# A scheduler of deferred VectorE work: a larger credit cap, no limit on tasks abreast, two shifted due times, more identity transposes ahead of the first product

## The chip, the cores and the metric

The kernel runs on one core of a Trainium2 chip. The metric is the device time of one execution in microseconds (us). TensorE (PE) multiplies, VectorE (DVE), ScalarE (ACT) and GpSimd (POOL) work beside it, each through its own queue in program order; PEld is TensorE's loading of weights. A stretch of the trace is given from the start of the profiled span.

## The reference

One encoder block on 256 tokens of width 4096, in float32. All weights are used once.

```
h = rms_norm(x, norm_gain); proj = h @ w_in            # 4096 -> 22528
q, k, v, z_attn, u_four, z_four, gates = split(proj)
o_attn = dilated window attention of 24 heads, merged over 3 groups by their log-sum-exp
branch_attn = (o_attn * silu(z_attn)) @ w_branch_attn  # 1024 -> 4096
y_four = real(fft2(u_four)) over tokens and group channels
branch_four = (y_four * silu(z_four)) @ w_branch_fourier   # 2048 -> 4096
mixed = sigmoid(g_attn) * branch_attn + sigmoid(g_four) * branch_four
out = rms_norm(x + mixed @ w_out, final_norm_gain)
```

## The kernel before, in words

**Products.** Every weight matrix is cut into column blocks of 512 (`gemm`). A block is worked off in steps of two 128-row slices: 16 steps where 4096 rows are summed. For a step, ScalarE copies 128x1024 weights to a rounded high half `wh`, and VectorE subtracts to get the low half `wl` (`split`). TensorE then does 12 products of 128x512 for the step: for each of two slices and two token tiles `wh` by the left side's high half, `wl` by its high half, `wh` by its low half. So each split of VectorE feeds four products with `wl`. Three pairs of `wh` and `wl` buffers rotate; the weights come by 1 MB transfers on SyncE's queue. In this text a **step** is one such split and its 12 products, and steps are counted from the kernel's first split.

**Deferred work.** Everything else that VectorE and ScalarE do (gates, rotary positions, softmax, 32x32 transposes, the folding of the left side for the Fourier branch, merging of the branches, final sums) is written as Python generators, the tasks. A task yields pairs (cost, delay): the VectorE time of its next piece in planned us, and the number of steps after which it may start. `step()`, called once per step between the split of the next step and the products of this one, hands out credit: `BUDGET` 1.45 (0.75 while the Fourier projection is interleaved, `BUDGET_U`), summed up to `CAP`. It walks through the list of tasks and issues pieces while credit lasts. This is done when the program is built: the result is a fixed order in each engine's queue. A piece of VectorE therefore stands between two splits, and all later splits queue behind it.

**Limits.** A task waits for the tasks named in its `after` list. Besides, `clock.abreast` lets the walk look only at so many tasks that are not urgent: 2 at first, 16 from the block `ZA0` to the end of the attention's transposes, 2 again for the merging.

**Due times.** `finish(...)` issues at once all that is left of given tasks. It is called for the attention heads (line 786) before the buffers of the attention are given up, and for the merging tasks within the first block of the last product, at its step 10 (line 865). In the merging stage each of eight column blocks has a block of products with `w_branch_attn` (4 steps) and one with `w_branch_fourier` (8 steps), and per token tile a task `transpose` that adds, transposes (16 instructions of 32x128), and splits the mixed rows `m` into `m_hi` and `m_lo`, which are the left side of the last product.

**Folding.** For the Fourier branch, `fold(b)` works on four 128-row slices of the left side: two pieces `f`, two pieces of an `e` pair, then ScalarE's `f_hi`, then VectorE's `f_lo`. The first three such tasks run before and within the first interleaved steps, five later ones follow further on. The interleaved projection itself adds, in a cycle of three steps, `wo` and `wu`, two `ul`, one `r` on VectorE, and two `uh` on ScalarE.

**Beginning.** Before the first product TensorE runs `warm(n)`: n transposes of an identity into an unused bank. Between them stand the four transposes of the first tiles of `x` and one of the gain.

Of the kernel before, what the change touches and what calls it, by code (L numbers as in the profile page):

```python
# [35 lines left out]
GA = (1, 3)  # L36
BUDGET = 1.45
BUDGET_U = 0.75
CAP = 1.5
ABREAST = 2  # L40
LEAD = 3

Q0, K0, V0, ZA0, U0, ZF0, G0 = 0, 3072, 6144, 9216, 10240, 12288, 14336
# [13 lines left out]
class Clock:  # L57
    now = 0
    budget = BUDGET
    abreast = ABREAST  # L60
    credit = 0.0


# [32 lines left out]
def hybrid_block(ctx: ExitStack, tc: tile.TileContext, x, norm_gain, w_in, gate_bias, w_attn,  # L96
# [3 lines left out]
    w_in, w_attn, w_four, w_out = w_in[0], w_attn[0], w_four[0], w_out[0]  # L100
# [34 lines left out]
    clock = Clock()  # L135
# [11 lines left out]
    def flush():  # L147

        while pending:
            pending.pop()()  # L150

    def finish(these):
        flush()
        complete(these)

    def complete(these):
        for t in list(these):
            complete(t.after)
            while t in tasks:
                if not t.run(clock.now):  # L160
                    tasks.remove(t)

    def step():
        clock.now += 1
        clock.credit = min(clock.credit + clock.budget, CAP)
        others = 0
        for t in list(tasks):
            if not t.urgent:
                others += 1
                if others > clock.abreast:  # L170
                    break
            if any(u in tasks for u in t.after):
                continue
            while t.ready <= clock.now and (t.cost <= clock.credit or clock.credit >= CAP):
                clock.credit -= t.cost
                if not t.run(clock.now):
                    tasks.remove(t)
                    break

    def split(src, hi, lo):  # L180
        act.activation(hi, src, AF.Copy)
        dve.tensor_tensor(lo, src, hi.bitcast(F32), op=ALU.subtract)
# [5 lines left out]
    def blocks(a):  # L188
        return a.rearrange("p (b k) -> p b k", k=P)
# [44 lines left out]
    def turn(name, shape, dtype):  # L234
        n = turns[name] = turns.get(name, -1) + 1
        if name == "wt":
            return wtp.tile(shape, dtype, name=f"wt{n % 3}")
        n %= 3 + len(spare)
        if n < 3:
            return wpool.tile(shape, dtype, name=f"{name}{n}")  # L240
        return lower(2 * spare[n - 3] + (name == "wl"), shape, dtype, f"{name}{n}")

    def gemm(accs, hi, lo, w, c0, lag=0, during=None, loading=None, at=None, between=None):

        nk = w.shape[0] // P
        wv = w[:, c0:c0 + CW].rearrange("(k p) n -> p k n", p=P)
        wt = None
        steps = []  # L250

        def load(k):
            nonlocal wt
            if k >= nk:
                return
            single = loading is not None and k == 0
            if k % WG == 0:
                wt = turn("wt", [P, WG, CW], F32)
                pieces = [(0, WG)] if not single else [(0, 1), (1, 2), (2, WG)]
                for a, b in pieces:  # L260
                    sp.dma_start(wt[:, a:b, :], wv[:, k + a:k + b, :])
                    if loading is not None:
                        loading(k + b)
            wh = turn("wh", [P, WS, CW], F32R)
            wl = turn("wl", [P, WS, CW], F32R)
            for j in range(0, WS, 1 if single else WS):
                n = slice(j, j + (1 if single else WS))
                split(wt[:, k % WG + n.start:k % WG + n.stop, :], wh[:, n], wl[:, n])
            steps.append((wh, wl))

        def multiply(i, j, t):
            if not 0 <= i < len(steps):
                return
            wh, wl = steps[i]
            k = i * WS + j
            a, b = hi[:, k, t * P:(t + 1) * P], lo[:, k, t * P:(t + 1) * P]
            pe.matmul(accs[t], a, wh[:, j, :], start=(k == 0), stop=False)
            pe.matmul(accs[t], a, wl[:, j, :], start=False, stop=False)
            pe.matmul(accs[t], b, wh[:, j, :], start=False, stop=(k == nk - 1))

        def run(i):
            load((i + 1) * WS)
            if during is not None:
                during(i * WS)
            if at is not None and i == at[0]:
                at[1]()
            step()
            for j in range(WS):
                for t in range(NT):
                    multiply(i - lag * t, j, t)  # L290
                if between is not None and j == 0:
                    between(i * WS)

        load(0)
        flush()
        if during is not None:
            during(-WS)
        last = nk // WS + lag - 1
        for i in range(last):
            run(i)  # L300
        pending.append(lambda: run(last))
# [62 lines left out]
    def warm(n):  # L364

        for _ in range(n):
            pe.transpose(idle_ps[:, :P], ident, ident)

    idle_ps = ps_mm.tile([P, CW], F32, name="acc10")
    x_load(0)  # L370
    warm(3)
    x_transposed(0)
    warm(6)

    def x_ahead(k):

# [290 lines left out]
    clock.budget = BUDGET  # L667


    clock.abreast = 16  # L670
    za = [new_accs()]
    gemm(za[0], h_hi, h_lo, w_in, ZA0, during=lambda k: u_hook(k) if k <= 12 else None)
    za.append(new_accs())
# [18 lines left out]
    with ExitStack() as st:  # L692
        ap = pool(st, "ap")
        at = pool(st, "at", bufs=2)
# [100 lines left out]
    with ExitStack() as st:  # L795
        ft = pool(st, "ft2")
        ys = [ft.tile([P, NT, CW], F32, name=f"yb{c}") for c in range(4)]
        for c in range(4):
            nc.gpsimd.dma_start(ys[c], y_d[:, :, c * CW:(c + 1) * CW].rearrange("t p n -> p t n"))

        def transposed(n, src, b, hi, lo):

            yield 0.0, 5 if n >= 4 else 0
            pt = ps_t.tile([P, 2, SEQ], F32, name="pt") if n % 2 else ps_s.tile([P, 2, SEQ], F32, name="sc")
            for j in range(2):
                for t in range(NT):
                    pe.transpose(pt[:, j, t * P:(t + 1) * P], src[:, t, (b + j) * P:(b + j + 1) * P], ident)
            yield 0.0, LEAD
            act.activation(hi, pt, AF.Copy)
            yield 0.7, 1  # L810
            dve.tensor_tensor(lo, pt, hi.bitcast(F32), op=ALU.subtract)

        flat = []
        for hi, lo, srcs in ((a_hi, a_lo, [sz]), (y_hi, y_lo, ys)):
            for k in range(0, hi.shape[1], 2):
                n = hi.shape[1] // len(srcs)
                flat.append(spawn(transposed(len(flat), srcs[k // n], k % n, hi[:, k:k + 2, :], lo[:, k:k + 2, :]),
                                  False, flat[-4:-3]))
        gates(2)
        finish(flat)  # L820
        clock.abreast = ABREAST


    m_hi, m_lo = lhs_parts("m")
    with ExitStack() as st:
        bp = pool(st, "bp", bufs=2)

        def scale_attn(ga, pa):
            for t in range(NT):
                yield 0.75, 0  # L830
                dve.tensor_mul(ga[:, t, 0, :], ga[:, t, 0, :], pa[t])

        def merge(c, ga, pf):
            for t in range(NT):
                yield 0.75, 0
                dve.tensor_mul(ga[:, t, 1, :], ga[:, t, 1, :], pf[t])

        def transpose(c, t, ga):
            yield 0.6, 0
            m = bp.tile([P, CW], F32, name="m")  # L840
            dve.tensor_add(m, ga[:, t, 1, :], ga[:, t, 0, :])
            mT = bp.tile([P, 4, P], F32, name="mT")
            yield from flipped(mT, blocks(m))
            yield from splitting(mT, m_hi[:, 4 * c:4 * c + 4, t * P:(t + 1) * P], m_lo[:, 4 * c:4 * c + 4, t * P:(t + 1) * P])

        merges, merging = [], []
        for c in range(8):
            if c > 2:
                complete(merges[c - 3])

            ga = sz.rearrange("p t (i n) -> p t i n", i=2) if c % 3 == 2 else bp.tile([P, NT, 2, CW], F32, name="ga")
            for i in range(2):
                nc.gpsimd.dma_start(ga[:, :, i, :], gates_d[:, :, i * D + c * CW:i * D + (c + 1) * CW].rearrange("t p n -> p t n"))
            accs = new_accs()
            gemm(accs, a_hi, a_lo, w_attn, c * CW)
            use(scale_attn(ga, accs))
            accs = new_accs()
            gemm(accs, y_hi, y_lo, w_four, c * CW)
            merged = use(merge(c, ga, accs))
            for t in range(NT):  # L860
                merging.append(spawn(transpose(c, t, ga), False, merged + merging[-2:-1]))
            merges.append(merging[-2:])

        first = new_accs()
        gemm(first, m_hi, m_lo, w_out, 0, at=(10, lambda: finish(merging)))

    br_stack.close()

# [108 lines left out]
```

## Time and profile before

| | |
|---|---|
| time, median of 3 | 2556.85 us (2555.99 to 2556.87) |
| profiled execution: its time | 2554.68 us |
| its span | 2552.9 us |
| TensorE busy | 2524.2 us, 99% of the span |
| VectorE busy | 1761.9 us, 69% |
| ScalarE busy | 1127.7 us, 44% |

The span is the profiled part of one execution; 1.8 us of that execution's time lie around it. The profiled execution was 2.2 us under the median of the others. All helper calls have one line in the trace (L54, the wrapper that records them in order), so rows are told apart by the tiles they write and read.

### The profile page before, as it was taken

How to read it: one execution, taken by the hardware profiler on the slowest of the kernel's cores; microseconds unless marked ns; L12 is line 12 of the kernel's file. 1: busy time of each engine (PE TensorE's matmuls, PEld its weight loads, DVE VectorE, ACT ScalarE, POOL GpSimd, SP SyncE). 2: the span in 40 equal slices, each digit the busy share in tenths (PEclk: the TensorE clock that was granted, in tenths of full speed). 3: DMA queues.
4: the chain of work that ended last, by engine and by line, in shares of the span. 5: the costliest groups of instructions: out<-in, count | busy, mean ns of one | idle time of the engine just before them, and what ended most of it. 6: DMA issues, size and time to landing. Idle time of an engine off the chain costs nothing.

```text
span 2552.9 us, 29910 instructions
## 1 busy us (share of the span) xinstructions
PE 2524.2 (99%) x11630; PEld 2103.2 (82%) x11630; DVE 1761.9 (69%) x2532; ACT 1127.7 (44%) x1352; POOL 77.8 (3%) x146
## 2 busy tenths in 40 slices
PE   9999999999999999999999999999999999899998
PEld 7888888888888888888888888888788888688886
DVE  5688877787754675757678775867756888754554
ACT  6645545454444434343444434344444444344443
POOL 0000000000001000000000000000000000000000
PEclk9999999999999999999999999999999999999999
DMA  7767666666655655565555555655666666566674
GB/s 253 249 231 241 237 228 238 235 231 215 222 173 173 202 189 192 198 195 189 186 185 186 189 188 195 198 178 194 229 228 219 207 221 201 174 196 223 218 243 149
DMA packets 252846, 529.60 MB, mean 207 GB/s; under 512 B 9984, under 2 KB 10784, under 8 KB 252704
## 3 DMA queue, kind: packets, MB, share of 16 engines
q1 hardware_dynamic: 237056, 471.89, 55.9%
q0 software_dynamic: 15600, 55.78, 6.5%
q8 instruction: 91, 1.49, 0.2%
q14 instruction: 51, 0.42, 0.0%
q10 hardware_dynamic: 48, 0.02, 0.0%
HBM read 512.97 MB, written 14.68 MB: 207 GB/s over the span
## 4 chain that ended last, share of the span: by engine, by line
PE 97%; DVE 1%; DMA 0%; ACT 0%; issue 0%; SPq 0%; DVEq 0%; ACTq 0%
PE acc L54 91%; PE pt L54 3%; PE sc L54 3%; DMA wt<-in_w_in_dram 0%; DVE mT L54 0%; DVE wl L54 0%; ACT wh L54 0%; DVE pT L54 0%; DVE res L54 0%; DVE h_lo L54 0%; ACT junk L54 0%; DVE m_lo L54 0%; DVE m L54 0%; ACT h_hi L54 0%; SPq L54 0%
## 5 line engine op out<-in xcount | busy, mean ns | idle before, releaser
L54 DVE TENSOR_TENSOR wl<-wt,wh 128x1024 fp32r<-128x1024 f32 (+1 forms) x865 | 1057.0, 1224 | 678.2 <-ACT wh L54 675.9
L54 ACT ACTIVATE wh<-wt 128x1024 fp32r<-128x1024 f32 (+1 forms) x865 | 912.9, 1059 | 1176.2 <-PE acc L54 1118.0
L54 PE MATMUL acc<-wh,h_hi 128*128 128x512 f32 x2560 | 1003.0, 392 | 0.9 <-ACT wh L54 0.9
L54 PE MATMUL acc<-wh,h_lo 128*128 128x512 f32 x2560 | 997.3, 390 | 0.0
L54 PE MATMUL acc<-wl,h_hi 128*128 128x512 f32 x2560 | 997.1, 389 | 0.1
L54 PEld LDWEIGHTS acc<-wh,h_lo 128*128 128x128 f32 x2560 | 481.0, 188 | 100.6
L54 PEld LDWEIGHTS acc<-wh,h_hi 128*128 128x128 f32 x2560 | 481.0, 188 | 97.1 <-ACT wh L54 1.3
L54 PEld LDWEIGHTS acc<-wl,h_hi 128*128 128x128 f32 x2560 | 481.1, 188 | 96.9 <-DVE wl L54 1.3
L54 PE MATMUL acc<-wh,m_hi 128*128 128x512 f32 x512 | 200.3, 391 | 9.2 <-ACT wh L54 9.2
L54 PE MATMUL acc<-wl,m_hi 128*128 128x512 f32 x512 | 200.2, 391 | 0.9 <-DVE wl L54 0.9
L54 PE MATMUL acc<-wh,m_lo 128*128 128x512 f32 x512 | 199.9, 390 | 0.0
L54 PEld LDWEIGHTS acc<-wh,m_hi 128*128 128x128 f32 x512 | 96.6, 189 | 29.6 <-ACT wh L54 9.6
L54 PEld LDWEIGHTS acc<-wl,m_hi 128*128 128x128 f32 x512 | 96.6, 189 | 22.0 <-DVE wl L54 1.8
L54 PEld LDWEIGHTS acc<-wh,m_lo 128*128 128x128 f32 x512 | 96.5, 189 | 20.1
L54 PE MATMUL acc<-wh,y_lo 128*128 128x512 f32 x256 | 101.2, 395 | 0.0
L54 PE MATMUL acc<-wl,y_hi 128*128 128x512 f32 x256 | 100.8, 394 | 0.0
L54 PE MATMUL acc<-wh,y_hi 128*128 128x512 f32 x256 | 100.0, 391 | 0.0
L54 DVE STREAM_TRANSPOSE mT<-m 32x128 f32<-32x128 f32 x256 | 77.4, 303 | 4.1
L54 DVE STREAM_TRANSPOSE pT<-e 32x128 f32<-32x128 f32 x256 | 77.2, 302 | 4.0
L54 DVE TENSOR_TENSOR ul<-wo,uh 128x508 fp32r<-128x508 f32 x64 | 44.0, 687 | 44.5 <-ACT uh L54 44.5
L54 ACT ACTIVATE uh<-wo 128x508 fp32r<-128x508 f32 x64 | 40.3, 630 | 71.4 <-DVE ul L54 71.4
L54 ACT ACTIVATE uh<-wu 128x516 fp32r<-128x516 f32 x64 | 40.9, 639 | 46.1 <-DVE wu L54 23.5
(151 smaller groups left out, 1679.3 us busy)
## 6 DMA issues: line engine op xcount, KB each, us to landing
wt<-in_w_in_dram SPq DMA_DIRECT2D x319, 1024.0 KB, 5.1
wt<-in_w_out_dram SPq DMA_DIRECT2D x64, 1024.0 KB, 5.5
wu<-in_w_in_dram POOLq DMA_DIRECT2D x64, 512.0 KB, 5.3
wt<-in_w_branch_fourier_dram SPq DMA_DIRECT2D x32, 1024.0 KB, 5.4
wt<-in_w_branch_attn_dram SPq DMA_DIRECT2D x16, 1024.0 KB, 5.5
gates_d<-sg POOLq DMA_DIRECT2D x32, 256.0 KB, 4.2
ga<-gates_d POOLq DMA_DIRECT2D x12, 512.0 KB, 5.3
bias<-in_gate_bias_dram SPq DMA_DIRECT2D x16, 256.0 KB, 5.5
```

The costliest lines, as they stand in the source:

```text
L54: return lambda *a, **k: self.tc.keep_in_program_order(f(*a, **k))
```

## The change

The credit of a step is kept up to 2.7 instead of 1.5. The limit on tasks abreast is gone: only the `after` lists hold a task back. The transposes of the Fourier rows become due 8 steps after they are spawned instead of 5. The forced end of the merging tasks stands at step 13 of the first block of the last product instead of step 10. At the beginning 14 and 40 identity transposes stand where 3 and 6 stood.

```
-CAP = 1.5
-ABREAST = 2
+CAP = 2.7
...
     budget = BUDGET
-    abreast = ABREAST
     credit = 0.0
...
         clock.credit = min(clock.credit + clock.budget, CAP)
-        others = 0
         for t in list(tasks):
-            if not t.urgent:
-                others += 1
-                if others > clock.abreast:
-                    break
             if any(u in tasks for u in t.after):
                 continue
             while t.ready <= clock.now and (t.cost <= clock.credit or clock.credit >= CAP):
...
     x_load(0)
-    warm(3)
+    warm(14)
     x_transposed(0)
-    warm(6)
+    warm(40)
...
-    clock.abreast = 16
...
-            yield 0.0, 5 if n >= 4 else 0
+            yield 0.0, 8 if n >= 4 else 0
...
-        clock.abreast = ABREAST
...
-        gemm(first, m_hi, m_lo, w_out, 0, at=(10, lambda: finish(merging)))
+        gemm(first, m_hi, m_lo, w_out, 0, at=(13, lambda: finish(merging)))
```

VectorE's queue, in the first block of the last product, from step 748 on (`wl` is a split, `mT` a transpose of merged rows), before:

```order
L54 TENSOR_TENSOR wl_16853<-wt_16850,wh_16852 128x1024
L54 STREAM_TRANSPOSE mT<-m 32x4x32 x4
L54 TENSOR_TENSOR wl_16873<-wt_16850,wh_16872 128x1024
L54 TENSOR_TENSOR m_lo<-mT,m_hi 128x4x128
L54 TENSOR_TENSOR m<-ga 128x512
L54 STREAM_TRANSPOSE mT<-m 32x4x32 x16
L54 TENSOR_TENSOR m_lo<-mT,m_hi 128x4x128
L54 TENSOR_TENSOR m<-ga 128x512
L54 STREAM_TRANSPOSE mT<-m 32x4x32 x16
L54 TENSOR_TENSOR m_lo<-mT,m_hi 128x4x128
L54 TENSOR_TENSOR wl_16935<-wt_16932,wh_16934 128x1024
```

The same place with the change:

```order
L53 TENSOR_TENSOR wl_16922<-wt_16899,wh_16921 128x1024
L53 STREAM_TRANSPOSE mT<-m 32x4x32 x4
L53 TENSOR_TENSOR wl_16944<-wt_16941,wh_16943 128x1024
L53 TENSOR_TENSOR wl_16961<-wt_16941,wh_16960 128x1024
L53 TENSOR_TENSOR m_lo<-mT,m_hi 128x4x128
L53 TENSOR_TENSOR wl_16980<-wt_16977,wh_16979 128x1024
```

Of the forced piece between two splits (32 transposes, two sums, three `m_lo`) one `m_lo` is left; the rest stands in earlier steps.

VectorE's queue at the end of the attention, steps 608 to 610 (`pT` is a transpose of the softmax rows, `e`, `mx`, `nm` the masked scores and their maximum), before:

```order
L54 TENSOR_TENSOR wl_13890<-wt_13887,wh_13889 128x1024
L54 STREAM_TRANSPOSE pT<-e_6789 32x4x32 x4
L54 TENSOR_TENSOR wl_13910<-wt_13887,wh_13909 128x1024
L54 STREAM_TRANSPOSE pT<-e_6789 32x4x32 x4
L54 TENSOR_TENSOR e_6790<-sc,mask_t 128x512
L54 TENSOR_REDUCE mx<-e_6790 128x1
L54 TENSOR_SCALAR nm<-mx 128x1
L54 SCALAR_TENSOR_TENSOR sz<-pt,rden_6795,sz 128x128
L54 RECIPROCAL rden_6796<-den_6793 128x1
L54 STREAM_TRANSPOSE pT<-e_6790 32x4x32 x16
L54 SCALAR_TENSOR_TENSOR sz<-pt,rden_6796,sz 128x128
L54 TENSOR_TENSOR wl_14010<-wt_14007,wh_14009 128x1024
```

The same place with the change:

```order
L53 TENSOR_TENSOR wl_13960<-wt_13941,wh_13959 128x1024
L53 SCALAR_TENSOR_TENSOR sz<-pt,rden_6841,sz 128x128
L53 TENSOR_TENSOR wl_13979<-wt_13976,wh_13978 128x1024
L53 TENSOR_TENSOR wl_13995<-wt_13976,wh_13994 128x1024
L53 TENSOR_TENSOR wl_14055<-wt_14052,wh_14054 128x1024
```

The last head's whole piece is gone from between the splits; the last `sz` is issued three steps earlier.

VectorE's queue in the folding, steps 46 to 48 (`f`, `e`, `f_lo` belong to the folding; `r`, `wo`, `wu`, `ul` to the interleaved projection), before:

```order
L54 TENSOR_TENSOR wl_1224<-wt_1221,wh_1223 128x1024
L54 TENSOR_SCALAR r_862<-wu_943,h_866 128x516
L54 TENSOR_TENSOR e<-f 128x4x63
L54 TENSOR_TENSOR e<-f 128x4x64
L54 TENSOR_TENSOR wl_1249<-wt_1221,wh_1248 128x1024
L54 TENSOR_TENSOR wo<-wu_945 128x508
L54 TENSOR_TENSOR wu_945<-wu_945 128x4x127
L54 TENSOR_TENSOR wl_1282<-wt_1279,wh_1281 128x1024
```

The same steps with the change:

```order
L53 TENSOR_TENSOR wl_1279<-wt_1276,wh_1278 128x1024
L53 TENSOR_SCALAR r_907<-wu_988,h_911 128x516
L53 TENSOR_TENSOR e<-f 128x4x63
L53 TENSOR_TENSOR e<-f 128x4x64
L53 TENSOR_TENSOR wl_1303<-wt_1276,wh_1302 128x1024
L53 TENSOR_TENSOR wo<-wu_990 128x508
L53 TENSOR_TENSOR wu_990<-wu_990 128x4x127
L53 TENSOR_TENSOR e<-f 128x4x63
L53 TENSOR_TENSOR e<-f 128x4x64
L53 TENSOR_TENSOR wl_1342<-wt_1339,wh_1341 128x1024
```

The third folding has moved forward by nine steps, so that it ends its `e` pieces in step 47 instead of step 56; the second has moved by six steps, from step 46 to step 40. Between the splits of steps 34 and 48 VectorE had four pieces `f`, four `e` pairs and one `f_lo`; it now has six `f`, six `e` pairs and two `f_lo`. ScalarE's `f_hi` follows the last `e` of a folding in the same step: twice in this stretch before (steps 39 and 46), three times now (37, 40 and 47).

## Rows read from the trace of the kernel before

**Rows 1.** The page, part 1: TensorE's busy time.

```profile
PE 2524.2 (99%) x11630; PEld 2103.2 (82%) x11630; DVE 1761.9 (69%) x2532; ACT 1127.7 (44%) x1352; POOL 77.8 (3%) x146
```

**Rows 2.** Busy time in three stretches of 25 us: PE first, granted clock before DMA share.

```profile
0.00:25.00 25.00, 21.66 (x93) 16.49 (x93) 11.89 (x20) 12.92 (x21) 0.69 (x6) 1.00 0.93 328
1800.00:1825.00 25.00, 22.30 (x115) 18.71 (x114) 20.18 (x44) 9.73 (x11) 3.06 (x5) 1.00 0.44 142
2200.00:2225.00 25.00, 15.32 (x62) 11.96 (x61) 22.19 (x51) 6.85 (x9) 0.00 (x0) 0.84 0.24 67
```

**Rows 3.** TensorE's waits, whole span: us in total, times, longest.

```profile
PE acc L54 <- ACT wh L54: 10.1, 2, 9.2
PE pt L54 <- DVE pT L54: 2.7, 1, 2.7
PE sc L54 <- PE acc L54: 0.9, 2, 0.6
```

**Rows 4.** Timeline of TensorE around 2212: start, duration, instruction, idle before.

```profile
2212.22 0.39 PE L54 MATMUL acc<-wh,m_lo 128*128 128x512 f32 x1
2221.82 0.80 PE L54 MATMUL acc<-wh,m_hi 128*128 128x512 f32 x1 [9.21 <-ACT wh L54]
...
2227.06 0.39 PE L54 MATMUL acc<-wl,m_hi 128*128 128x512 f32 x1
2227.29 0.39 PE L54 MATMUL acc<-wh,m_lo 128*128 128x512 f32 x1
```

**Rows 5.** Timeline of VectorE in the same stretch.

```profile
2208.04 5.05 DVE L54 STREAM_TRANSPOSE mT<-m 32x128 f32<-32x128 f32 x16
```

**Rows 6.** Timeline around 1818, TensorE.

```profile
1818.39 1.16 PE L54 MATMUL pt<-v,pT 128*128 128x128 f32 x8 [2.69 <-DVE pT L54]
```

**Rows 7.** Timeline of the beginning, TensorE.

```profile
1.36 0.90 PE L54 MATMUL acc<-ident 128*128 128x128 f32 x3 [1.36 <-POOL ident masks.py:199]
...
4.85 1.54 PE L54 MATMUL acc<-ident 128*128 128x128 f32 x6
...
7.25 0.80 PE L54 MATMUL acc<-wh,h_hi 128*128 128x512 f32 x1 [0.86 <-ACT wh L54]
...
9.43 0.63 PE L54 MATMUL acc<-wl,h_hi 128*128 128x512 f32 x1
...
11.89 0.39 PE L54 MATMUL acc<-wh,h_lo 128*128 128x512 f32 x1
...
14.20 1.04 PE L54 MATMUL pt<-ident,xt 128*128 128x128 f32 x8
```

**Rows 8.** VectorE's groups from 103 to 116.6: busy, mean ns, idle before.

```profile
L54 DVE TENSOR_TENSOR wl<-wt,wh 128x1024 fp32r<-128x1024 f32 x5 | 6.1, 1226 | 3.3 <-ACT wh L54 3.3
```

**Rows 9.** Timeline of VectorE in the folding (splits of steps 40 and 48).

```profile
115.43 0.75 DVE L54 TENSOR_TENSOR e<-f 128x252 f32<-128x252 f32 x2
118.32 1.23 DVE L54 TENSOR_TENSOR wl<-wt,wh 128x1024 fp32r<-128x1024 f32 x1 [2.13 <-ACT wh L54]
119.46 1.22 DVE L54 TENSOR_TENSOR f_lo<-e,f_hi 128x1024 fp32r<-128x1024 f32 x1
...
143.11 1.22 DVE L54 TENSOR_TENSOR wl<-wt,wh 128x1024 fp32r<-128x1024 f32 x1
```

**Rows 10.** Timeline of TensorE: the first product that reads the split of step 48.

```profile
145.97 0.39 PE L54 MATMUL acc<-wl,h_hi 128*128 128x512 f32 x1
```

**Rows 11.** Timeline: the split of step 89, and the first product that reads it.

```profile
272.02 1.23 DVE L54 TENSOR_TENSOR wl<-wt,wh 128x1024 fp32r<-128x1024 f32 x1 [0.83 <-ACT wh L54]
...
277.83 0.39 PE L54 MATMUL acc<-wl,h_hi 128*128 128x512 f32 x1
```

**Rows 12.** Timeline of VectorE at the first final sum, steps 759 and 760.

```profile
2246.29 0.68 DVE L54 TENSOR_TENSOR res<-res,acc 128x512 f32<-128x512 f32 x1
...
2248.72 1.23 DVE L54 TENSOR_TENSOR wl<-wt,wh 128x1024 fp32r<-128x1024 f32 x1 [0.26 <-ACT wh L54]
```

**Rows 13.** Timeline of TensorE: the first product that reads the split of step 760.

```profile
2252.24 0.39 PE L54 MATMUL acc<-wl,m_hi 128*128 128x512 f32 x1
```

## The prediction

> **What bounds the kernel now.** I read the page's busy times first. TensorE is busy 2524.2 of 2552.9 us [rows 1], so at most 28.7 us can be won without taking products away. The next question is where these lie. I cut the span into stretches of 25 us, and only a few are not full: the beginning (3.3 us idle), 1800 to 1825 (2.7), 2200 to 2225 (9.7) [rows 2]; with the 0.9 us named next, the other 12 us lie in the last stretches. The list of waits names causes: 10.1 us in two waits for the high halves `wh` of the weights, one of them 9.2 us, 2.7 us in one wait for `pT`, and 0.9 us before the transposes of the Fourier rows [rows 3]. The end is a chain that the change leaves as it is. So the case is about four places, and the rest of the kernel can only get worse.
>
> The reader should see in the two long waits that the engine named is not the cause. At 2212 VectorE works for 5.05 us on 16 transposes in a row, and does the same again behind that [rows 5]; ScalarE's copy `m_hi` waits for them, the next `wh` copies queue behind it, and TensorE starves [rows 4]. It is the work that the forced end of the merging tasks lays between two splits. At 1818 it is the last attention head, forced likewise [rows 6].
>
> **The merging burst.** The product at 2212.22 is followed by one at 2221.82, and the eleventh after it starts at 2227.06 [rows 4]. At full pace products start every 0.23 us (2227.06 to 2227.29); eleven would have taken 2.5 us, and took 14.84. **The burst costs 12.3 us**: the wait of 9.2, and slow products behind it: the granted clock is 0.84 in that stretch of 25 us [rows 2]. TensorE fell from 2.4 to 1.2 GHz after it had stood, and rose 5.2 us after it took up work. In the changed queue one `m_lo` is left of this piece. The other work has gone forward, at most into steps with a few transposes each; VectorE's splits have slack there (below). I take the whole 12.3 as gained. The bounds are 9.2 (the wait alone) and 12.3. The forced end at step 13 instead of 10 finds nothing to do in the changed order: nothing.
>
> **The attention burst.** The wait of 2.69 us [rows 6] goes, since no head is left to be forced: **2.7 us gained**, between 2.0 and 2.7.
>
> **Transposes of the Fourier rows, due three steps later.** They waited 0.9 us in all, for VectorE to read the bank they overwrite [rows 3]. With the change three `y_lo` stand in one step directly ahead of the transposes that need their banks, where two stood. One wait falls away, another grows by a `y_lo`. Zero, from a loss of 0.9 to a gain of 0.9.
>
> **The folding.** Here the change lays more work into early steps. Price by price [rows 9]: an `f` or `f_lo` holds VectorE 1.14 us (as the split of the same shape does, 118.32 to 119.46), an `e` pair 0.7; the last `e` pair of a folding is dearer, for the next split starts 2.89 us after it (115.43 to 118.32): ScalarE's `f_hi` waits for `e`, the next `wh` waits behind `f_hi`, and VectorE idles 2.13 us for that `wh`. Between the splits of steps 34 and 48 the changed queue has two more `f`, two more `e` pairs, one more `f_lo`, and one more `f_hi` wait: 2 x 1.14 + 2 x 0.7 + 1.14 + 2.2 = 7.0 us. VectorE had idle time there, 3.3 us over five splits [rows 8]. Chained from split 34 on with these prices, VectorE comes to the split of step 37 some 0.5 us before its `wh` is there, so 2.8 us are absorbed. The split of step 48 comes 4.2 us later than at 143.11, and ends at 148.5. TensorE read it at 145.97 [rows 10], only 1.6 us after its old end of 144.33. **TensorE stalls by about 2.5 us** near 146, in small part at step 41, where four `e` pieces stand together. I take 2.4. The ends are 0 (the tasks are hidden after all) and 4.2 (no slack left from earlier steps).
>
> The five later foldings also start two `f` in one step, but there VectorE's lead is long, and no second folding follows close: the split of step 89, where the second of the five starts, begins at 272.02, ends at 273.25, and is read at 277.83, 4.6 us later [rows 11]. A second `f` (1.14), two `e` pairs (1.4) and the `f_hi` wait (2.1), with two or three steps between in which VectorE regains some of it, stay just below that. I cost them at nothing; without that lead each would cost like the first group, up to 4.2 us.
>
> **Rotary, attention and merging.** Bursts grow by one or two pieces of 0.7 us (for instance two maskings in a step), less than the lead even where it was shortest of these, 2.3 us at step 760 [rows 12, 13]: nothing. The tightest place is that final sum: all four pieces of a block come into one step, so that split 760, which starts at 2248.72, 2.43 us after the first sum [rows 12], waits for a second sum and square, some 2.1 us more: it then ends at about 2252.05, and TensorE reads it at 2252.24 [rows 13]. So nothing, with 0.2 us to spare, at each of seven places; up to 1 us in all.
>
> **The beginning.** Six identity transposes in a row take 1.54 us, three take 0.90, so one more costs 0.21 us [rows 7]. The clock column says 1.00 for the first 25 us [rows 2], yet a product of 512 columns takes 0.63 us at 9.43, and 0.39 from 11.89 on as everywhere later [rows 7]: TensorE was at 1.2 GHz until about 11.6, some 4.3 us after its dense work began at 7.25; after the burst it took 5.2 us. Put that on the change. Fourteen transposes, four of `x` and one of the gain from 1.36 on end at about 5.6; if this dense work counts like products, the clock rises at 5.7 to 6.6. Then three of the forty are done at 0.21, and 37 at half of that (eight take 1.04 at 14.20, about 0.11 each [rows 7]): 4.0 us. The first product starts at 10.2 instead of 7.25, at 2.4 GHz. Until 14.20 the kernel before did 24 products and four transposes; 24 x 0.23 + 0.44 = 6.0 us, so the changed one is there at 16.2. **The beginning loses 2.0 us.** It can't lose less than 1.7 (all forty at 0.11), and not more than 6.9 (all at 0.21: 8.5 us from 5.6 to 14.1, and the first products slow again). Nothing behind it takes this up: the left sides of this block come from later transposes of `x`, which shift with TensorE.
>
> The Trainium skill ("TensorE: Matmul & The Clock Gate", Part 4: PE-mode transpose) says that the full clock does not engage for transposes, since they do not count as busy time in the same way. By that rule the beginning would cost the upper end; no row of this trace decides it, for the early transposes stood with gaps and the clock rose only within products.
>
> **Sum.** 12.3 + 2.7 - 2.4 - 2.0 = 10.6 us less than the profiled execution's 2554.68: 2544.1. The median of before stands 2.2 higher, so its counterpart is **2546.3 us**.
>
> **The rivals.**
> - *Transposes don't lift the clock.* The forty run at 0.21 us each and the first products are slow as before: 6.6 us lost instead of 2.0, time 2550.9. For it: the clock rose only 4.3 us into dense products. Against it: nothing in these rows. This is the rule named above.
> - *Folding hidden.* ScalarE takes `f_hi` sooner than I chain it, or the work spreads: no stall; 2543.9, and 2543.6 if the beginning costs its least. For it: the early foldings passed without a wait that the list names [rows 3]. Against it: only 1.6 us of lead at step 48 [rows 9, 10].
> - *Slower.* The five later foldings stall as well: two `f` in one step, then `e` and `f_hi` in interleaved steps whose `ul` wait for ScalarE too. At 4.2 us each this is 21 us, time 2567. From 3.2 us each it makes the kernel slower by over 5 us. Against it: the lead when a folding starts [rows 11].
> - *The change doesn't do what it says:* the credit is kept, but bursts return at another forced end. The order of instructions speaks against it; time about 2556 to 2560.
>
> **How the numbers follow.** Forecast 0.44 (2544 to 2549 with the bounds of folding and beginning); no clock from transposes 0.32; folding hidden 0.14; slower 0.04; no effect 0.03; a mixture 0.03. About 0.2% (5.1 us) is what a measurement of this kernel can tell from no change; faster by more means under 2551.7. The forecast and the hidden folding lie below, and about two thirds of the second case, as 2550.9 is close to the bound: 0.80 faster, 0.16 the same, 0.04 slower. The range 2541.5 to 2552 takes in the first three cases.
>
> **What the profile would show.** Right: no wait over 3 us of TensorE between 1800 and 2230, granted clock 1.00 there; a wait of about 2 us for `wl` or `wh` near 146; the first product of 512 columns near 10, its followers 0.23 us apart. Wrong: a first product near 14 (the first rival); waits behind `e` or `f_hi` from 200 to 430 (the third); waits at the final sums from 2240 on, behind ScalarE's squares.

## The result, and the profile after

The changed kernel takes **2541.91 us** in the median of five executions (2541.61 to 2542.03), against 2556.63 us for the kernel before in the same session (six executions, 2554.99 to 2557.22). The ratio is 0.9943, with a 95% interval of 0.9929 to 0.9957: 0.57% faster, 14.7 us. A further execution of the changed kernel took 3629.51 us with TensorE's mean granted clock at 0.65; it is left out. The profiled execution took 2541.89 us (span 2540.1), 12.8 us less than that of before (2554.68).

The page's busy times, and TensorE's waits over the whole span (us in total, times, longest):

```profile
PE 2524.5 (99%) x11675; PEld 2106.8 (83%) x11675; DVE 1759.8 (69%) x2532; ACT 1129.1 (44%) x1352; POOL 77.5 (3%) x146
```

```profile
PE acc L53 <- DVE wl L53: 1.7, 3, 0.8
PE acc L53 <- POOL ident masks.py:199: 1.4, 1, 1.4
PE sc L53 <- PE acc L53: 0.5, 1, 0.5
PE acc L53 <- ACT wh L53: 0.4, 1, 0.4
```

TensorE and VectorE do as much as before [rows 1]; what is gone is idle time. The waits of 9.2 us for `wh` and of 2.7 us for `pT` [rows 3] are not in the list any more, the largest left in the middle of the kernel is 0.8 us, and new ones for `wl` have come. Stretches of 25 us (PE busy first, granted clock before DMA share) say where they stand:

```profile
0.00:25.00 25.00, 23.64 (x132) 20.54 (x133) 11.52 (x20) 11.95 (x21) 0.69 (x6) 1.00 0.93 329
50.00:75.00 25.00, 24.42 (x112) 19.83 (x111) 13.66 (x15) 22.56 (x51) 0.00 (x0) 1.00 0.53 172
125.00:150.00 25.00, 23.52 (x114) 19.09 (x112) 21.37 (x28) 11.21 (x16) 1.08 (x2) 1.00 0.65 218
1800.00:1825.00 25.00, 25.00 (x124) 21.02 (x124) 12.43 (x12) 10.40 (x10) 4.84 (x7) 1.00 0.89 309
2200.00:2225.00 25.00, 25.00 (x112) 20.71 (x111) 13.62 (x17) 10.43 (x11) 0.00 (x0) 1.00 0.69 236
```

Two of these stretches were full before:

```profile
50.00:75.00 25.00, 25.00 (x115) 20.66 (x114) 14.20 (x14) 22.26 (x51) 0.00 (x0) 1.00 0.60 198
125.00:150.00 25.00, 25.00 (x129) 21.45 (x128) 20.83 (x27) 13.32 (x18) 1.28 (x3) 1.00 0.61 199
```

The two stretches with the bursts [rows 2] are full now, at full clock. 125 to 150 has lost 1.5 us, at the place that I had predicted, and 50 to 75 has lost 0.6, which I had not foreseen.

Idle time alone does not show products that run slowly. So I took, for each step, the start of the first product that reads its split, once before and once after. The difference, after less before, is the lag of TensorE at that step; where it changes for good, time was lost or won. (The first step's split comes as two half splits, and each is counted.)

| from step to step | place | lag, us | change |
|---|---|---|---|
| 0 to 16 | beginning | 0 to 0.82 | +0.8 |
| 16 to 18 | squares of `x` | 0.82 to 1.72 | +0.9 |
| 40 to 60 | folding | 1.71 to 3.86 | +2.15 |
| 480 to 622 | end of attention, Fourier transposes | 3.84 to 0.12 | -3.7 |
| 749 to 752 | merging | 0.15 to -12.23 | -12.4 |
| 760 to 850 | final sums of six blocks | -12.22 to -12.09 | +0.1 |
| 850 to 860 | final sums of the seventh | -12.09 to -12.82 | -0.7 |

Between steps 410 and 622 the lag also swings by up to 2.8 us and comes back, because the attention's small products and the Fourier transposes stand at other places in TensorE's queue; at steps 480 and 622 both kernels have done the same number of them. Everywhere else the lag stands still.

### The profile page after: what moved, and what is told of

Read it like the earlier page. It is cut to its first block, busy times and chain, and to the rows that moved or that the text cites. A ratio compares the mean times of both kernels' runs of the same rounds, so it can differ in the third digit from the quotient of the medians.

```text
span 2540.1 us, 29998 instructions
## 1 busy us (share of the span) xinstructions
PE 2524.5 (99%) x11675; PEld 2106.8 (83%) x11675; DVE 1759.8 (69%) x2532; ACT 1129.1 (44%) x1352; POOL 77.5 (3%) x146
## 4 chain that ended last, share of the span: by engine, by line
PE 96%; DVE 2%; ACT 1%; DMA 1%; issue 0%; SPq 0%; DVEq 0%; ACTq 0%
PE acc L53 90%; PE pt L53 3%; PE sc L53 3%; DVE wl L53 1%; ACT wh L53 1%; DMA wt<-in_w_in_dram 1%; DMA xt<-in_x_dram 0%; DVE h_lo L53 0%; DVE f L53 0%; DVE e L53 0%; ACT h_hi L53 0%; SPq L53 0%; ACT junk L53 0%; DVE res L53 0%; DVE ul L53 0%
```

## The rows behind that account

**Merging.** VectorE where the forced piece stood [rows 5]:

```profile
2206.93 0.68 DVE L53 TENSOR_TENSOR m_lo<-mT,m_hi 128x512 fp32r<-128x512 f32 x1
2208.49 1.23 DVE L53 TENSOR_TENSOR wl<-wt,wh 128x1024 fp32r<-128x1024 f32 x1 [0.88 <-ACT wh L53]
2211.16 1.23 DVE L53 TENSOR_TENSOR wl<-wt,wh 128x1024 fp32r<-128x1024 f32 x1 [1.45 <-ACT wh L53]
```

One `m_lo` of 0.68 us is left of it, and VectorE now waits for `wh`: the ring of `wh` and `wl` is paced by TensorE again.

**Folding.** VectorE around the split of step 48, then TensorE's products of that step:

```profile
145.74 0.75 DVE L53 TENSOR_TENSOR e<-f 128x252 f32<-128x252 f32 x2
148.62 1.23 DVE L53 TENSOR_TENSOR wl<-wt,wh 128x1024 fp32r<-128x1024 f32 x1 [2.13 <-ACT wh L53]
```

```profile
148.64 0.50 PE L53 MATMUL acc<-wh,h_hi 128*128 128x512 f32 x1 [0.40 <-ACT wh L53]
149.90 0.51 PE L53 MATMUL acc<-wl,h_hi 128*128 128x512 f32 x1 [0.76 <-DVE wl L53]
```

The last `e` pair and the 2.13 us for `wh` behind it are those of [rows 9], now directly ahead of split 48. That split ends at 149.85 and TensorE reads it at 149.90: the lead of 1.6 us [rows 10] is used up.

**Squares.** ScalarE in step 16, the first and the last rows of what stands there between two `wh`:

```profile
53.13 1.05 ACT L53 ACTIVATE wh<-wt 128x1024 fp32r<-128x1024 f32 x1
54.08 0.40 ACT L53 ACTIVATE junk<-xt 128x256 f32<-128x256 f32 x1
...
55.69 0.42 ACT L53 ACTIVATE junk<-xt 128x256 f32<-128x256 f32 x1
...
57.48 1.05 ACT L53 ACTIVATE wh<-wt 128x1024 fp32r<-128x1024 f32 x1
```

```profile
59.85 0.50 PE L53 MATMUL acc<-wl,h_hi 128*128 128x512 f32 x1 [0.58 <-DVE wl L53]
```

`norms` yields a planned 1.35 for each pair of squares. These are ScalarE's, yet they are paid with VectorE's credit. At a cap of 1.5 one pair passed per step; at 2.7, which is twice 1.35, two pass, and the second `wh` comes 4.35 us after the first. The splits are used every 2.72 us, and the next one is late.

**Final sums.** VectorE at the first of them, then TensorE's first reading of the split behind it:

```profile
2236.15 0.68 DVE L53 TENSOR_TENSOR res<-res,acc 128x512 f32<-128x512 f32 x1
2237.67 0.69 DVE L53 TENSOR_TENSOR res<-res,fg 128x512 f32<-128x512 f32 x1 [0.84 <-ACT junk L53]
2238.62 3.69 DVE L53 TENSOR_TENSOR wl<-wt,wh 128x1024 fp32r<-128x1024 f32 x3 [0.26 <-ACT wh L53]
```

```profile
2240.02 0.39 PE L53 MATMUL acc<-wl,m_hi 128*128 128x512 f32 x1
```

All four pieces are in one step; the first of the three splits ends at 2239.85, 0.17 us before it is read. The spare 0.2 us of the prediction held.

**Beginning.** TensorE's first rows:

```profile
1.35 3.25 PE L53 MATMUL acc<-ident 128*128 128x128 f32 x14 [1.35 <-POOL ident masks.py:199]
4.40 1.06 PE L53 MATMUL pt<-ident,xt 128*128 128x128 f32 x4
5.39 0.31 PE L53 MATMUL sc<-ident,gr 32*128 32x32 f32 x1
5.63 5.12 PE L53 MATMUL acc<-ident 128*128 128x128 f32 x40
10.50 0.48 PE L53 MATMUL acc<-wh,h_hi 128*128 128x512 f32 x1
...
15.17 1.03 PE L53 MATMUL pt<-ident,xt 128*128 128x128 f32 x8
```

The forty take 0.128 us each in the mean, where 0.21 is the pace at 1.2 GHz and 0.11 that at 2.4 [rows 7]; the granted clock rose at 6.76, among them. The first product of 512 columns runs at full clock. The eight transposes of `x` start at 15.17 instead of 14.20.

## The experiments

Lags below are always against the profiled execution of the kernel before. The kernel before was run with each group of experiments, and its medians there were 2556.86 (e1 to e4, 19 executions), 2554.96 (e5 to e8, 9) and 2555.38 us (e9 to e11, 19). In all it scattered from 2553.85 to 2558.39.

### e1: the cap alone

```
-CAP = 1.5
+CAP = 2.7
```

> The kernel before with one edit: the credit cap 2.7 instead of 1.5. Theory (the gain is the two forced bursts, and the cap alone spreads them): both bursts are gone, the beginning is the old one (0.85 us shorter than in the changed kernel), the stalls of the folding (2.2 us) and at the squares (0.9 us) are there: span about 2539.3 us, time about 2541, ratio 0.994. Rival (the limit on tasks abreast held the merging back): the wait near 2212 stays in large part, time about 2548 or more.

Measured: 2542.58 us (2541.94 to 2543.57), ratio 0.9946 (0.9931 to 0.9961), span 2540.1. Both bursts are gone, the lag rises by 0.9 at the squares and by 2.2 at the folding, and ends at -12.75, nearly that of the whole change (-12.82). **The cap is the change**: of the other edits, the identity transposes cost 0.8 to 0.9 us, the later due time of the Fourier transposes gives 1.0 (e7), and the two cancel. The span is 0.8 us above the expectation and the median 1.6: it had counted the old beginning, but not the old due time. The Fourier transposes, still due at 5, wait as before:

```profile
PE sc L54 <- PE acc L54: 0.9, 2, 0.6
```

### e2: no limit on tasks abreast, alone

```
-                if others > clock.abreast:
-                    break
```

> The kernel before with one edit: no limit on tasks abreast, cap 1.5. Theory: the attention's forced end is untouched (wait 2.7 us near 1818), the merging's forced piece is 8.7 us of VectorE's work instead of 14.4; TensorE waits about 3.5 to 4 us there instead of 9.2, and the clock need not fall: 8 us won, time about 2548. Rival (the limit is the cause): nearly all of the change's gain, time about 2542.

Measured: 2551.28 us (2548.1 to 2552.16), ratio 0.9978 (0.9969 to 0.9987). The merging piece is smaller, and its wait is 3.5 us instead of 9.2; the attention's stays whole:

```profile
PE acc L54 <- ACT wh L54: 4.4, 2, 3.5
PE pt L54 <- DVE pT L54: 2.7, 1, 2.7
```

The expectation missed by 3 us: the clock fell behind both waits (at 1818.4 and 2217.7), and the products after them were slow. At the first this cost 1.5 us (lag 0.26 to 1.75). At the second the lag fell by 5.0, where the shorter wait alone gives 5.7: the slow products of the long burst are all still there, and cost 0.7 us more.

### e3: the identity transposes alone

```
-    warm(3)
+    warm(14)
...
-    warm(6)
+    warm(40)
```

> The kernel before with one edit: 14 and 40 identity transposes at the beginning. Theory: the first product of 512 columns starts at 10.5 at 2.4 GHz, the kernel is 0.85 us later from there to its end: time about 2557.5, ratio 1.0003. Rival (the transposes give the part of the gain that the bursts don't explain): about 2 us faster, 2554.6.

Measured: 2557.01 us (2555.07 to 2558.33), ratio 1.0001 (0.9991 to 1.001). The lag is 0.8 from step 16 to the end; the transposes bring nothing.

### e4: the changed kernel, with the cap at 1.5 until the folding is over

```
+    cap = 1.5
...
-        clock.credit = min(clock.credit + clock.budget, CAP)
+        clock.credit = min(clock.credit + clock.budget, clock.cap)
...
     clock.budget = BUDGET
+    clock.cap = CAP
```

> The changed kernel with the cap at 1.5 until the last of the interleaved blocks is issued, 2.7 from there on. Theory (the cap costs 2.2 us at the foldings and 0.9 us at the squares): no wait of TensorE over 0.3 us between 50 and 200, span about 2537, time about 2538.9, ratio to before 0.993. Rival (the stalls come from the transposes' later start or from the missing limit on tasks): same time as the changed kernel, 2541.9.

Measured: 2538.74 us (2538.45 to 2538.98), ratio 0.9931 (0.9916 to 0.9945): 3.2 us better than the change. The stretch from 125 to 150 is full:

```profile
125.00:150.00 25.00, 25.00 (x125) 21.26 (x125) 20.71 (x28) 12.67 (x18) 1.08 (x2) 1.00 0.63 214
```

The lag at step 480 is 0.96 instead of 3.84. Squares and folding were real losses, both made by the cap.

### e5 and e6: e4 with 14 and 14, and with 3 and 6 identity transposes

```
-    warm(40)
+    warm(14)
```

and for e6

```
-    warm(14)
+    warm(3)
...
-    warm(40)
+    warm(6)
```

> As the kernel with the cap raised after the folding, but 14 and 14 identity transposes at the beginning. Theory (the transposes do lift the clock, and 40 of them hold TensorE 2.5 us past the time when the first split is ready): the first product starts near 8.0 to 8.3 instead of 10.5 and is followed every 0.23 us; span about 2535, time about 2536.6. Rival (fewer transposes let the clock rise only within the products): the products start near 8.2 but slow, nothing won or lost against the old 3 and 6: about 2537.8.

> As the kernel with the cap raised after the folding, with the old 3 and 6 transposes. Theory (40 transposes cost 0.9 us net): span about 2536.2, time about 2537.8, with the clock rising after 11. Rival (the transposes pay): 2539.5 or more.

Measured: 2538.26 us (2537.97 to 2539.09) for e5 and 2538.30 us (2538.24 to 2539.38) for e6, both 0.9932 (0.9919 to 0.9944). e5's expectation missed by 1.7 us. TensorE in e5:

```profile
5.63 1.83 PE L53 MATMUL acc<-ident 128*128 128x128 f32 x14
8.03 0.50 PE L53 MATMUL acc<-wh,h_hi 128*128 128x512 f32 x1 [0.57 <-ACT wh L53]
...
20.28 0.50 PE L53 MATMUL acc<-wl,h_hi 128*128 128x512 f32 x1 [0.76 <-DVE wl L53]
```

The clock rose at 5.84, and the first product stands at 8.03 at full clock. At step 3 TensorE is 0.95 us ahead of the kernel before, but at step 5 (20.28) it waits for the split and is 0.14 us behind. What TensorE gains ahead of that it gives back there: here VectorE and ScalarE set the pace of the first steps. So 9, 28 or 54 transposes differ by under 1 us. The lag at step 16 was 0.8 to 1.0 with 54 of them (five kernels), 0.1 with 28, and from -0.1 to 0.8 with the old nine (six kernels besides the one before), so that single values of it mean little.

### e7: the changed kernel with the old due times

```
-            yield 0.0, 8 if n >= 4 else 0
+            yield 0.0, 5 if n >= 4 else 0
...
-        gemm(first, m_hi, m_lo, w_out, 0, at=(13, lambda: finish(merging)))
+        gemm(first, m_hi, m_lo, w_out, 0, at=(10, lambda: finish(merging)))
```

> The changed kernel with the Fourier transposes due after 5 steps and the forced end of the merging at step 10, as before. Theory (the later due time of the Fourier transposes saves up to 0.9 us of waits near 1845, the forced end finds nothing either way): span about 2541.0, time 2542.8, ratio to the changed kernel 1.0004, all of it between 1820 and 1870. Rival (a due time is what keeps a burst away): a wait of over 2 us near 1840 or 2205.

Measured: 2542.63 us (2542.47 to 2542.87), ratio 0.9948 (0.9936 to 0.9961). The final lag is -11.84 instead of -12.82, and the 0.98 us between them arise from step 609 to 622, at the Fourier transposes; their waits are 0.9 us in two, where the changed kernel has one of 0.5. So 0.4 us of the 0.98 are idle time that the list names; the rest was not taken apart. The forced end at 10 or 13 makes no difference once nothing is left to force.

### e8 and e10: the larger cap in the merging alone, and in the attention alone

Both are the kernel before with a `clock.cap` of 1.5 that is 2.7 in one part only, set for e8 in the line behind the merging's `clock.abreast = ABREAST`, for e10 behind the interleaved projection, and taken back in that line of the merging:

```
-        clock.credit = min(clock.credit + clock.budget, CAP)
+        clock.credit = min(clock.credit + clock.budget, clock.cap)
...
+        clock.cap = 2.7
```

> The kernel before with one edit: the cap is 2.7 from the end of the Fourier transposes on. The merging burst goes, the attention's wait of 2.7 us stays. Theory (the clock falls after that wait in some executions and not in others, and this is why the runs of before scatter by 3 us and lie 2 us above the profiled one): span 2539.7 to 2540 when the clock holds, 1.5 us more when it falls; times scatter from 2541.5 to 2543.5. Rival (the scatter comes from the burst near 2212): all runs within 0.5 us near 2541.6.

> The kernel before, with the credit cap at 2.7 only from the end of the interleaved projection to the end of the attention. The forced end of the last head finds nothing left; the forced piece of the merging stays at 14.35 us of VectorE work. Theory: the wait of 2.7 us for pT near 1818 is gone, and with it the fall of the clock that follows it in most executions: the profiled times drop by 2.7 to 3, and all executions lie within 1 us of each other, near 2552, while the wait of 9 us near 2212 stays. Rival: the scatter of the kernel before comes from the wait at 2212 (its fall of the clock sooner or later): then the executions still scatter over 2 to 3 us, from 2551.5 to 2554.5.

e8: 2544.11 us, ratio 0.9952 (0.9938 to 0.9965); its five executions are 2541.72, 2543.86, 2544.11, 2544.28 and 2544.51. In the profiled one TensorE behind the attention's wait reads so:

```profile
1819.21 1.99 PE L54 MATMUL pt<-v,pT 128*128 128x128 f32 x8 [2.69 <-DVE pT L54]
1820.99 1.06 PE L54 MATMUL sc<-ident,sz 128*128 128x128 f32 x4
```

Eight products take 1.99 us, against 1.16 behind the same wait before [rows 6]; the clock fell at 1819.33 and rose at 1822.74, and the lag went from 0.82 to 2.47. So the fall behind this wait comes in some executions and not in others, and costs 1.65 us in this one. By their times four of the five have it; these lie 2.1 to 2.8 us above the fifth, more than the 1.5 that I expected and up to 1.0 us above the range, and what makes the rest was not taken apart.

e10: 2552.76 us (2551.37 to 2553.06, ten executions), ratio 0.9988 (0.9979 to 0.9998). The wait for `pT` is gone, the other stays, and the lag falls by 2.8:

```profile
PE acc L54 <- ACT wh L54: 10.1, 2, 9.2
```

The profiled time fell by 3.0 us (2554.68 to 2551.65), as expected; the median lies 0.8 us above the 2552 of the theory. The kernel before in the same group has two clusters of times, ten from 2554.41 to 2555.38 and nine from 2556.26 to 2558.39; the times of e10 form one, and scatter by 1.7 us instead of 4.0. So more than half of the scatter belonged to the attention's wait. I had expected 1 us, and the 1.7 do not show that the merging's wait has a share, as the rival said: e1, with neither wait and the same nine transposes at the beginning, scatters by 1.6.

### e9: the changed kernel, one pair of squares in a step

```
-            yield 1.35, 0
+            yield 1.36, 0
```

> The changed kernel, with the planned cost of a pair of squares of x raised from 1.35 to 1.36 us, just above half of the cap: each pair then stands in a step of its own, as it did before; VectorE's bursts of the folding and of all later places stay as in the changed kernel. Theory: two pairs in one step make the split of that step 0.86 us late and nothing takes this up later, so the first reading of the splits from step 17 on comes 0.85 us later than before the change (the beginning alone) in place of 1.7, the folding then adds its 2.2 as always, and the time is 2541.9 - 0.9 = 2541.0. Rival: the folding's stall is set by VectorE alone, so that what is won at step 17 is lost again at step 48: 0.85 us at step 18, but 3.9 us again at step 60, and 2541.9 as with the change.

Measured: 2540.73 us (2540.56 to 2541.03), ratio 0.9942 (0.993 to 0.9955). The stretch of the squares is full:

```profile
50.00:75.00 25.00, 25.00 (x115) 20.64 (x115) 14.56 (x15) 22.55 (x50) 0.00 (x0) 1.00 0.56 188
```

The lag stays at 0.93 from step 17 to 40, rises by 2.2 in the folding as in the changed kernel, and ends at -13.65, 0.83 less. The rival, that the folding takes it all back, is out.

### e11: the later forced end alone

```
-        gemm(first, m_hi, m_lo, w_out, 0, at=(10, lambda: finish(merging)))
+        gemm(first, m_hi, m_lo, w_out, 0, at=(13, lambda: finish(merging)))
```

> The kernel before, with the forced end of the merging at step 13 of the first block of the last product instead of 10. The forced piece moves from step 749 to step 752 and shrinks from 14.35 to 11.76 us of VectorE work. Theory: TensorE's wait there is the piece less a fixed lead, so it shrinks by the same 2.6 us, from 9.2 to about 6.6, the slow products behind it stay (3.1 us), and the time is 2.6 us less: 2552.1 for an execution like the profiled one, 2554.2 in the median. Rival: the piece is needed in any case before the second block's left side, so a later forced end meets a shorter lead and the wait stays at 9: 2556.8 in the median.

Measured: 2562.14 us (2561.22 to 2563.72), ratio 1.0026 (1.0016 to 1.0035): **slower by 6.8 us**, against both theories. TensorE's three long waits there:

```profile
2219.92 0.50 PE L54 MATMUL acc<-wh,m_hi 128*128 128x512 f32 x1 [1.46 <-ACT m_hi L54]
...
2226.99 0.80 PE L54 MATMUL acc<-wh,m_hi 128*128 128x512 f32 x1 [5.83 <-ACT m_hi L54]
...
2239.86 0.80 PE L54 MATMUL acc<-wh,m_hi 128*128 128x512 f32 x1 [5.92 <-ACT wh L54]
```

The piece is smaller, but the products of step 752, for the one token tile and then for the other, read the very `m_hi` that it has yet to make, so TensorE waits for the whole of it. Then the weights are missing. ScalarE, and SyncE's queue:

```profile
2238.76 2.00 ACT L54 ACTIVATE wh<-wt 128x1024 fp32r<-128x1024 f32 x2 [10.88 <-DMA wt<-in_w_out_dram]
```

```profile
2227.73 0.34 SPq L54 DMA_DIRECT2D fg<-in_final_norm_gain_dram  x1
2228.12 0.90 SPq L54 DMA_DIRECT2D res<-in_x_dram  x2
2229.06 13.54 SPq L54 DMA_DIRECT2D wt<-in_w_out_dram  x4
```

The loads of `fg` and `res` stand in that queue ahead of the next weights. They are issued at 2227.73, after the last `m_lo` of the piece has begun, against 2221.62 in the kernel before; all later weights come behind them. For which buffer they wait was not taken apart. The step of the change that looks harmless is so only because the cap has emptied the forced end.

## Why the prediction was right, and where it was off

The forecast case came out: 2546.3 us predicted, 2541.91 measured, inside the range and just above its lower end. It lies 2.1 us below the 2544 to 2549 that I had given to this case, and that it still falls within the range is in part luck: the lower end of 2541.5 was set with the hidden folding in view, which did not come. Of the 4.4 us between, half is the step from the profiled execution to the median, half are terms.

- **From 2544.1 to 2546.3, failed.** I added the 2.2 us by which the median of before stood above its profiled execution. The changed kernel has no such step (2541.89 profiled, 2541.91 in the median): it belonged to waits that the change removes. Behind the attention's wait the clock falls in some executions, at 1.65 us in e8 and 1.5 in e2; the profiled executions of before, e3 and e11 have the same wait without the fall. With this wait the times of before form two clusters, without it those of e10 form one. How much of the 2.2 us that explains stays open: in the group of e10 the medians lie 2.6 us apart, no more than the wait itself. Without both waits the executions of the four kernels with 54 transposes (the changed one, e4, e7, e9) agree within 0.6 us, those with 9 or 28 (e1, e5, e6) within 1.1 to 1.6; that the beginning makes this difference was not tested.
- **Merging, 12.3: right** (12.4). The wait alone would have been 9.2; to count the slow products behind it was worth 3 us.
- **Attention, 2.7, and Fourier transposes, 0: together 3.7.** The mechanism held. The attention gave 2.8 of it, and the transposes due later 1.0 (e7), just beyond the upper bound of 0.9 that I had named; I took the middle of the bounds.
- **Folding, -2.4: right** (-2.15), at the steps named, 41 and 48. "Folding hidden" is out. The slower rival is out as well: from step 60 to 410 the lag is constant, and the five later foldings, the last of which ends in step 167, cost nothing.
- **Beginning, -2.0: mis-sized** (-0.8, less than the 1.7 that I had called the least; over all kernels with 54 transposes the lag at step 16 is 0.65 more in the mean than with nine). The clock rose among the transposes, at 6.76 where I had 5.7 to 6.6, and the first product came at 10.50 where I had 10.2. The error is the count of what stood ahead of 14.20: 18 products and four transposes, not 24. The changed kernel is there at 15.17, not at 16.2. Beyond that, in e5 the wait for VectorE's split at step 5 took an early start back.
- **The clock rule, a rival at 0.32: refuted here.** TensorE was at 2.4 GHz before the first product of 512 columns, with nothing but float32 transposes behind it. The Trainium skill ("TensorE: Matmul & The Clock Gate", Part 4: PE-mode transpose) says that the full clock does not engage for transposes; its times there are for bf16. For these float32 transposes the trace disagrees (6.76 us against the first product at 10.50), and the same in e3 (5.70, first product at 9.99) and e5 (5.84, first product at 8.03).
- **Not seen: the squares, -0.9,** shown by e9. I had looked through the changed order for larger bursts of VectorE; ScalarE's work, released by the same credit, delays `wh` and so the split as well.
- **Final sums: 0, right, with 0.2 us to spare as predicted. Not seen: the seventh block, +0.7.** Before, the sums of that block stood in two steps and TensorE waited 0.41 us for a split at 2511; now there is no wait. Why that block alone had waited was not tested.

The two terms that I had not seen, squares and seventh block, nearly cancel. The terms add to 12.8 us against the predicted 10.6.

## What to carry to other kernels

When a scheduler spreads small work between the splits of a steady stream, look at the largest piece between two splits, not at the mean load: the cap alone turned some 14 us of VectorE work between two splits into small pieces and gave the gain, and where the consumer's lead is short (the folding, the squares) the same cap costs 3 us, so it belongs to a stage and not to the whole program (2538.3 to 2538.7 in e4 to e6, better than both kernels). Bound what one step may release on every engine in the chain to the split: the squares had their price in the plan, and two pairs still passed at once on ScalarE because the cap allowed it. A forced end moved later can cost more than it saves, when the products behind it read what it makes (e11). When the profiled execution and the median differ, ask first whether the difference hangs on a wait that the change removes.

## What was not expected of the hardware

TensorE's clock behind the same wait of 2.69 us stayed at 2.4 GHz in the profiled executions of before, e3 and e11 and fell to 1.2 GHz in those of e2 and e8; there eight products of 128x128 took 2.08 and 1.99 us instead of 1.16. A wait's price is then its length plus a part that differs from execution to execution. At the beginning the clock rose with the same dense transposes between 5.70 us (e3) and 7.15 us (e4) in the profiled executions of five kernels, so the forty took 4.60 us in e3 and 5.12 in the changed kernel.
